# Gate columns moved into the value projection of a RetNet/HGRN2 layer, with the head norm along the free axis and a transpose at the end

## The chip, the cores and the metric

The kernel runs on one core of one Trainium2 chip. The metric is the device time in microseconds (us) of one execution. A NeuronCore has several engines that run side by side: PE (TensorE, the matrix products; PEld is the same engine loading the weights that stay put while the other operand moves), ACT (ScalarE), DVE (VectorE), POOL (GpSimd) and SP (SyncE, which here issues the DMAs). Products accumulate in PSUM banks; ACT and DVE read them from there ("evacuate" them) into SBUF.

## The reference

One layer of a hybrid decoder over 2048 prompt tokens and 64 sample tokens (8 sequences of 8 tokens, with a carried state), width 1024:

```python
proj = h @ w_in                       # h = rmsnorm(x); 8 parts of 512 columns
rq, rk, rv, rg, hq, hf, hi, hg = split(proj)
# four retention heads: rotary on rq, rk; chunked recurrence with a fixed decay
o_r, s_ret_new = chunk_gla(rq, rk, rv, log_gamma, s_ret)
o_r = head_rmsnorm(o_r, ret_norm_w) * silu(rg)
# four HGRN2 heads: f = lb + (1-lb) sigmoid(hf), k = 1-f, q = silu(hq)/sqrt(dk)
o_h, s_hg_new = chunk_gla(hq, 1 - f, hi, log(f), s_hg)
o_h = head_rmsnorm(o_h, hgrn_norm_w) * silu(hg)
x = x + concat([o_r, o_h]) @ w_out
x = x + square(relu(rmsnorm(x) @ w_up)) @ w_down        # d_ff = 4096
y = rmsnorm(x)
```

`head_rmsnorm(o, w)` is `o * rsqrt(mean(o*o over the head's 128 values) + 1e-6) * w`. The outputs are y and the new states of all heads, for the prompt and for each sample sequence.

## The kernel before, in words

**Precision.** Every float32 product is made of three products of a faster format: each operand is split into a high and a low part, and high x high, high x low and low x high are accumulated. A weight block is 128 x 1024 values (1024 = 8 blocks of 128 columns). `weight` (L244) loads a raw block from DRAM, ACT copies the high part (L270) and DVE subtracts for the low part (L284). The input and output projections' blocks from the fifth on are stored in DRAM as parts by the first group (`next_weight`, stores at L318) and loaded as parts by the other two (L253). Raw blocks have 3 buffers, blocks used by the Strassen sums 4 of their own tag, parts 3 pairs. `self.ahead` is 2: at a block's use the next two are begun.

**Stages.** The 2112 tokens are cut into three groups (L41) of 640, 768 and 704 tokens (64 of samples and 640 of the prompt). Each group is mixed in turn: 0 to 350 us, 350 to 760 and 760 to 1188 us. The feed-forward part of all three follows, to the end, with Strassen-Winograd products (L1211) whose weight sums are made during the mixing of groups 1 and 2 (`plan_sums`, L1232; loads L1240, stores L1248).

**Mixing.** `mix` (L623) runs over four pairs p, each of one retention and one HGRN2 head. For each it emits: the gates of the pair before (`gates`, L664); the projections f, q, rq, rk (`project`, L674); the recurrence (`mixer`, L860, by an agenda); and the values (`values`, L717). Gates and projections keep the weights still and move the tokens: a block gives a tile [128 columns of w_in x T tokens], in two halves of T/2 tokens (L341). A gate is evacuated by DVE with the row norm, sigmoided by ACT (with loads of an activation table before and after) and multiplied. The values keep a 128-token chunk still and move the weights: 8 x 3 matmuls of 256 columns (both heads' 128, L748) per chunk. For the 64 sample tokens the two high products share one stationary tile, whose lower half holds the low part of the tokens; the lower rows are then moved by a DMA and added (16 matmuls, L742, L744). Up to three chunks share a PSUM tile; ACT evacuates a chunk with the token's norm factor as the scale (L758).

**Order.** Engine orders come from the emission order and a tile scheduler. `at`, `later` and `tick` (L206 to L222) form an agenda: `tick` is called once per few matmuls of projections and values, and what is due is emitted between them. `mixer` puts its steps at written offsets: scores by levels of blocks, then per chunk `outputs` (L1100, L1102) and `states` (L1108, L1115) 7 ticks apart. In the last group the sample sequences come ahead of the chunks: `sample_states` (L769) loads 4 states per buffer and two buffers per head, `sample_out` (L781, L784) multiplies, `sample_update` (L835, L839, L842, L843) makes the new states and stores them from the same buffers. The load buffers (`ld`, 6) also hold cos and sin for a whole group and the low copies.

**Head norm and output.** Outputs lie as [128 values x tokens], in one PSUM bank per segment and head. `gate_norm` (L1183) squares on ACT (L1188), splits the squares, multiplies output by gate (L1190), sums over the 128 partitions by two matmuls with a tile of ones (L511, L512), takes rsqrt on ACT (L357, L358) and multiplies (L1196). `cut_heads` (L1199) splits the gated heads in two parts, which `residual` (L1216) and `out_proj` (L1262) use as the moving operand of the output projection. PSUM: two double banks `pj` for projections and values, four banks `mm` for all small products.

Of the kernel before, what the change touches and what calls it, by code (L numbers as in the profile page):

```python
# [9 lines left out]
F32 = mybir.dt.float32  # L10
F32R = mybir.dt.float32r
# [18 lines left out]
NSLAB = 44  # L30
NLD = 6
# [19 lines left out]

N_MADE = 4
# [94 lines left out]
def in_blocks():  # L147
    for p in range(H):
        if p:
            yield from ((7, p - 1), (3, p - 1))  # L150
        yield from ((5, p), (4, p), (0, p), (1, p), ("v", p))
    yield from ((7, H - 1), (3, H - 1))


def lay_out_weights(w_in, w_out, w_up, w_down):
# [3 lines left out]
    for part, p in in_blocks():  # L159
# [4 lines left out]
        for half in range(2):  # L164
            b = wi[half * 4:half * 4 + 4][:, :, (2, 6), p]
            w[i] = b.transpose(1, 0, 2, 3).reshape(P, WT)
            i += 1
# [32 lines left out]
class Kernel:  # L200
# [43 lines left out]
    def weight(self, i):  # L244
        n = len(self.stream)
        while self.w_next < min(i + 1 + self.ahead, n):
            j = self.w_next
            e = self.stream[j]
            if e[0] == "p":

                self.wts[j] = tuple(self.wp.tile([P, WT], F32R, tag=tag, name=tag) for tag in ("hi", "lo"))
# [16 lines left out]
            hi = self.wp.tile([P, WT], F32R, tag="hi", name="hi")  # L268
            lo = self.wp.tile([P, WT], F32R, tag="lo", name="lo")
# [353 lines left out]
    def mix(self, g):  # L623
# [6 lines left out]
        prev = None  # L630
        end = 0
        for p in range(H):
            b = {}
            if prev is not None:
                self.gates(g, prev)
            self.project(g, p, b)
            end = self.mixer(g, p, b, max(self.now, end))
            self.values(g, p, b)
            prev = b
        for p in range(H - 1):  # L640
            self.later(2 + 18 * p, self.cut_heads, g, p)
        self.gates(g, prev)
# [21 lines left out]
    def gates(self, g, b):  # L664

        for key, col in (("gh", V_HN), ("gr", V_RN)):
            z = self.normed(g, self.block(g))
            sg, q = self.get(), self.get()
            self.sigmoid(sg[:, :g.T], z)
            b[key] = q  # L670
            self.later(5, lambda q=q, z=z, sg=sg, col=col: self.nc.vector.scalar_tensor_tensor(
                out=q[:, :g.T], in0=z, scalar=self.vec[:, col:col + 1], in1=sg[:, :g.T], op0=ALU.mult, op1=ALU.mult))
# [44 lines left out]
    def values(self, g, p, b):  # L717

        nc = self.nc
        w = [self.next_weight(), self.next_weight()]  # L720
        b["vs"], b["vc"] = None, []

        left = -(-len(g.starts) // 3)
        i1 = 0
        while left:
            i0, i1 = i1, i1 - (i1 - len(g.starts)) // left
            left -= 1
            part = g.starts[i0:i1]
            pj = self.pj.tile([P, 2, 512], F32, tag="pj", name="pjv").rearrange("p a b -> p (a b)")
            v = self.get()  # L730
            for i, s in enumerate(part):
                for kb in range(KB):
                    hh, hl = g.h[kb]
                    cols = slice((kb % 4) * 256, (kb % 4 + 1) * 256)
                    wh, wl = w[kb // 4][0][:, cols], w[kb // 4][1][:, cols]
                    if g.ns and s == 0:

                        dst = pj[:, i * 256:(i + 1) * 256]
# [8 lines left out]
                    for q, (a, ww) in enumerate(((hh, wh), (hh, wl), (hl, wh))):  # L747
                        nc.tensor.matmul(pj[:, i * 256:(i + 1) * 256], a[:, s:s + C], ww,  # L748
                                         start=kb == 0 and q == 0, stop=kb == KB - 1 and q == 2)
                    self.tick()  # L750
                pair = (v[:, i * 256:i * 256 + P], v[:, i * 256 + P:(i + 1) * 256])
# [1076 lines left out]
```

## Time and profile before

| | us |
|---|---|
| median of 3 runs | 2494.79 (2494.51 to 2495.32) |
| span of the profiled execution | 2490.7 |
| what lies around the span, by the median | 4.1 |
| mixing of group 0, 1, 2 | 350, 410, 428 |
| feed-forward part | 1302 |

In the profile a row of a view that groups instructions reads: line, engine, operation, output<-input by the program's names, partitions x elements, count, then busy time and the mean or the min/median/max in ns of one. In the chain of work that ended last, a row is start, length, engine, tile and line, with the count of instructions in that piece. A row of DMA issues ends with the median time from issue to landing in us. In the timeline, "x2" means that two instructions of the kind follow each other in that row. Matmuls overlap on PE, so that their durations add up to more than the time that they take.

### The profile page before, as it was taken

What the parts mean: (1) busy time and instruction counts of PE and PEld (TensorE: products, weight loads), DVE (VectorE), ACT (ScalarE), POOL (GpSimd) and SP (SyncE); (2) the same over time, 40 slices, a digit from 0 to 9 for tenths busy, and PEclk for the clock granted to TensorE, in tenths of its full rate; (3) what the DMA queues carried; (4) which work ended last, traced back from release to release, by engine and by line L of the source; (5) the groups of instructions that cost most, each with busy time, mean ns of one, the idle gap of its engine ahead of it and who ended that gap; (6) DMA issues with size and microseconds to landing.
All of it is one profiled execution on the core that took longest, in us unless ns stands there. A gap on an engine that the chain in (4) does not pass through costs nothing.

```text
span 2490.7 us, 41430 instructions
## 1 busy us (share of the span) xinstructions
PE 2478.4 (100%) x16520; PEld 2461.9 (99%) x16520; DVE 1868.8 (75%) x2453; ACT 1246.4 (50%) x1674; POOL 377.3 (15%) x320
## 2 busy tenths in 40 slices
PE   9999999999999999999999999999999999999998
PEld 9999999999999999999999999999999999999998
DVE  7666766667685666686775899776699878778987
ACT  6665663444464444453644545444454436445544
POOL 5223304324421442340000000000000000000000
PEclk9999999999999999999999999999999999999999
DMA  7454575465566665768876866576675545867552
GB/s 265 166 185 170 203 259 178 161 229 186 184 210 236 220 219 200 266 211 270 283 213 221 280 198 213 174 239 222 203 262 177 188 151 190 288 196 247 194 189 89
DMA packets 191655, 525.44 MB, mean 211 GB/s; under 512 B 20963, under 2 KB 62563, under 8 KB 191462
## 3 DMA queue, kind: packets, MB, share of 16 engines
q1 hardware_dynamic: 191318, 522.77, 62.3%
q8 instruction: 130, 2.13, 0.4%
q14 instruction: 63, 0.52, 0.1%
q10 hardware_dynamic: 144, 0.02, 0.0%
HBM read 389.28 MB, written 132.39 MB: 209 GB/s over the span
## 4 chain that ended last, share of the span: by engine, by line
PE 98%; DVE 1%; DMA 0%; ACT 0%; issue 0%; SPq 0%; DVEq 0%
PE pj L341 29%; PE pf L1211 26%; PE pj L1211 25%; PE pjv L748 8%; PE mm L920 2%; PE mm L1108 1%; PE po L1100 1%; PE po L1102 1%; PE mm L977 1%; PE mm L512 1%; PE mm L511 1%; PE po L784 1%; PE mm L1034 1%; PE mm L850 1%; DMA lo<-w33lo 0%; DMA slab<-x 0%
## 5 line engine op out<-in xcount | busy, mean ns | idle before, releaser
L270 ACT CAST hi<-raw 128x1024 fp32r<-128x1024 f32 x392 | 411.8, 1050 | 616.6 <-PE pf L1211 258.4
L341 PE MATMUL pj<-slab,hi 128*128 128x320 f32 (+2 forms) x3072 | 661.4, 328 | 1.8 <-DVE slab L649 1.0
L1211 PE MATMUL pf<-slab,hi 128*128 128x320 f32 (+2 forms) x2768 | 657.6, 321 | 0.0
L1211 PE MATMUL pj<-slab,hi 128*128 128x352 f32 (+2 forms) x2608 | 620.6, 322 | 0.0
L284 DVE TENSOR_TENSOR lo<-raw,hi 128x1024 fp32r<-128x1024 f32 x392 | 485.6, 1239 | 113.6 <-ACT hi L270 108.1
L341 PEld LDWEIGHTS pj<-slab,hi 128*128 128x128 f32 x3072 | 508.3, 188 | 3.9 <-DVE slab L649 1.2
L1211 PEld LDWEIGHTS pf<-slab,hi 128*128 128x128 f32 x2768 | 480.1, 188 | 0.0
L1211 PEld LDWEIGHTS pj<-slab,hi 128*128 128x128 f32 x2608 | 452.9, 188 | 0.1
L1211 PE MATMUL pf<-slab,lo 128*128 128x320 f32 (+2 forms) x1384 | 444.1, 321 | 0.0
L1211 PE MATMUL pj<-slab,lo 128*128 128x352 f32 (+2 forms) x1304 | 419.1, 321 | 0.0
L341 PE MATMUL pj<-slab,lo 128*128 128x320 f32 (+2 forms) x1536 | 379.5, 327 | 0.5 <-DVE lo L284 0.4
L341 PEld LDWEIGHTS pj<-slab,lo 128*128 128x128 f32 x1536 | 263.6, 188 | 1.6 <-DVE lo L284 1.0
L1211 PEld LDWEIGHTS pf<-slab,lo 128*128 128x128 f32 x1384 | 259.6, 188 | 0.0
L1211 PEld LDWEIGHTS pj<-slab,lo 128*128 128x128 f32 x1304 | 244.6, 188 | 0.0
L748 PE MATMUL pjv<-hi,slab 128*128 128x256 f32 x1024 | 193.3, 285 | 0.0
L1302 ACT CAST slab<-slab 128x640 fp32r<-128x640 f32 (+2 forms) x192 | 145.2, 778 | 64.0 <-DVE slab L1313 51.7
L1306 DVE TENSOR_TENSOR slab<-slab 128x640 fp32r<-128x640 f32 (+2 forms) x192 | 167.0, 884 | 8.5 <-PE pj L1211 2.8
L748 PEld LDWEIGHTS pjv<-hi,slab 128*128 128x128 f32 x1024 | 162.2, 192 | 1.4
L748 PE MATMUL pjv<-lo,slab 128*128 128x256 f32 x512 | 144.8, 283 | 0.0
L899 ACT ACTIVATE slab<-slab 128x640 f32<-128x640 f32 (+2 forms) x72 | 56.3, 782 | 147.7 <-POOL slab L895 147.4
L1556 DVE TENSOR_TENSOR slab<-pf,slab 128x640 f32<-128x640 f32 (+2 forms) x88 | 77.5, 886 | 29.4 <-PE pf L1211 28.9
L748 PEld LDWEIGHTS pjv<-lo,slab 128*128 128x128 f32 x512 | 98.1, 192 | 0.0
(222 smaller groups left out, 3009.0 us busy)
## 6 DMA issues: line engine op xcount, KB each, us to landing
raw<-w SPq DMA_DIRECT2D x264, 512.0 KB, 4.3
slab<-u SPq DMA_DIRECT2D x32, 384.0 KB, 4.8
u<-ld SPq DMA_DIRECT2D x30, 384.0 KB, 4.0
slab<-u SPq DMA_DIRECT2D x32, 352.0 KB, 5.0
u<-ld SPq DMA_DIRECT2D x30, 352.0 KB, 3.9
slab<-u SPq DMA_DIRECT2D x32, 320.0 KB, 4.6
u<-ld SPq DMA_DIRECT2D x30, 320.0 KB, 4.3
ld<-x SPq DMA_DIRECT2D x16, 384.0 KB, 3.8
```

The source lines that it names most:

```text
L270: self.nc.scalar.copy(hi, raw)
L284: self.nc.vector.tensor_tensor(out=lo, in0=self.second.pop(j), in1=hi.bitcast(F32), op=ALU.subtract)
L341: self.nc.tensor.matmul(pj[:, i, :T2], w, a[:, c0:c1], start=j == 0 and q == 0, stop=j == n - 1 and q == 2)
L511: self.nc.tensor.matmul(ps, self.ones_r, hi, start=True, stop=False)
L512: self.nc.tensor.matmul(ps, self.ones_r, lo, start=False, stop=True)
L748: nc.tensor.matmul(pj[:, i * 256:(i + 1) * 256], a[:, s:s + C], ww, start=kb == 0 and q == 0, stop=kb == KB - 1 and q == 2)
L899: nc.scalar.activation(x["dd", w][:, a:T], x["dd", w][:, a:T], AF.Exp)
L920: nc.tensor.matmul(ps[:, j], qk[:, cols[c]], second(qk[:, cols[c]]), start=True, stop=True)
L1211: self.nc.tensor.matmul(*a, **k)
L1302: self.nc.scalar.copy(hi[:, :g.T], B[name][:, :g.T])
L1306: self.nc.vector.tensor_tensor(out=lo[:, :g.T], in0=B[name][:, :g.T], in1=hi.bitcast(F32)[:, :g.T], op=ALU.subtract)
L1556: nc.vector.tensor_tensor(out=r, in0=ps, in1=r, op=ALU.add)
```

## The change

- The weights are laid out anew: a pair's value blocks hold 512 columns per 128 rows (value and gate of both heads), four blocks per pair instead of two (`N_VAL`), and the two gate blocks are gone. The count of blocks stays.
- `values` moves 512 columns in place of 256. Two chunks share a `pj` tile. ACT evacuates values and gates with two copies per chunk. The sample chunk's lower rows are moved and added for values and gates.
- `gates` works on [tokens x gate columns] slabs: sigmoid as Exp, Ln, Exp on ACT (no table load), then a product on DVE.
- `outputs` and `sample_out` swap their operands, so that outputs lie as [tokens x 256 (both heads)]; two chunks share a bank of `mm`.
- The head norm sums squares along the free axis: ACT Square with an accumulated sum per token (`squares`), Ln and Exp on a [128, 2, 2] tile (`factors`), one DVE operation per chunk and head that multiplies output, factor and gate (`gated`).
- `cut_heads` transposes the gated heads back by PE, 128 x 128 at a time; ACT and DVE make the parts from PSUM with the norm's weight as the scale. Heads 0 to 2 are cut 50, 65 and 80 ticks after the last `mixer` is begun.
- Buffers: slabs 44 to 43, load buffers 6 to 5, raw weight blocks 3 + 4 to 4 of one tag, part pairs 3 to 5.

The diff, cut:

```diff
-NSLAB = 44
-NLD = 6
+NSLAB = 43
+NLD = 5
+NRAW = 4
+NPART = 5
+N_VAL = 4
 def in_blocks():
     for p in range(H):
-        if p:
-            yield from ((7, p - 1), (3, p - 1))
         yield from ((5, p), (4, p), (0, p), (1, p), ("v", p))
-    yield from ((7, H - 1), (3, H - 1))
...
-                k, later = self.w_load, self.w_load >= self.n_sums
-                other = later and k % 7 % 2
-                raw = self.raws[k] = self.wp.tile([P, WT], F32, tag="sum" if other else "raw", name="raw",
-                                                  bufs=4 if other else 3)
+                raw = self.raws[k] = self.wp.tile([P, WT], F32, tag="raw", name="raw", bufs=NRAW)
...
-            if prev is not None:
-                self.gates(g, prev)
             self.project(g, p, b)
             end = self.mixer(g, p, b, max(self.now, end))
+            if p == H - 1:
+                for q in range(H - 1):
+                    self.later(50 + 15 * q, self.cut_heads, g, q)
             self.values(g, p, b)
...
+    def gates(self, slab, n, first):
+        nc, sg = self.nc, self.get()
+        z, e = slab[:, :n], sg[:, :n]
+        self.later(first, lambda: nc.scalar.activation(e, z, AF.Exp, scale=-1.0))
+        self.later(first + 3, lambda: nc.scalar.activation(e, e, AF.Ln, bias=1.0))
+        self.later(first + 6, lambda: nc.scalar.activation(e, e, AF.Exp, scale=-1.0))
+        self.later(first + 11, lambda: nc.vector.tensor_tensor(out=z, in0=z, in1=e, op=ALU.mult))
...
+        ahead, self.ahead = self.ahead, NPART - N_VAL
+        w = [self.next_weight() for _ in range(N_VAL)]
+        self.ahead = ahead
...
+        for j0 in range(0, n, 2):
+            pj = self.pj.tile([P, 2, 512], F32, tag="pj", name="pjv")
...
+                    cols = slice((kb % 2) * 512, (kb % 2 + 1) * 512)
...
+                        nc.tensor.matmul(dst, a[:, s:s + C], ww, start=kb == 0 and q == 0, stop=kb == KB - 1 and q == 2)
+                        if q != 1:
+                            self.tick()
...
-        nc.tensor.matmul(po[:, :NS], v, AT, start=True, stop=False)
+        nc.tensor.matmul(po, AT, v, start=True, stop=False)
...
-                nc.tensor.matmul(dst, b["vc"][c][hd], am(i, c), start=True, stop=first)
+                nc.tensor.matmul(dst, am(c), b["vc"][c][hd], start=True, stop=first)
                 if not first:
-                    nc.tensor.matmul(dst, S, qd[:, cols[c]], start=False, stop=True)
+                    nc.tensor.matmul(dst, qd[:, cols[c]], S, start=False, stop=True)
...
+        def squares(k, i, c, r=slice(0, P)):
+            o, _ = place(c)
+            for hd in range(2):
+                a = hd * P
+                nc.scalar.activation(o[r, a:a + P], x["po", k][r, i * 256 + a:i * 256 + a + P], AF.Square,
+                                     accum_out=x["ss", k][r, hd, i:i + 1])
...
+        for c in range(n):
+            two, i = divmod(c, 2)
+            at(t + 6, outputs, c)
+            at(t + chunk, states, c)
+            at(t + 9, squares, two, i, c)
+            if i or c == n - 1:
+                at(t + 9, factors, two, i + 1)
+                for d in range(i + 1):
+                    at(t + 13 + d, gated, two, d, c - i + d)
+            t += chunk
...
     def cut_heads(self, g, p):
...
+                    nc.tensor.transpose(ps[:, s:s + n], o[:n, c:c + P], self.ident[:n, :n])
+                self.tc.keep_in_program_order(nc.scalar.activation(hi[:, a:e], ps, AF.Copy, scale=w))
+                nc.vector.scalar_tensor_tensor(out=lo[:, a:e], in0=ps, scalar=w, in1=hi.bitcast(F32)[:, a:e],
+                                               op0=ALU.mult, op1=ALU.subtract)
```

More of the change, by code (lines that the diff above doesn't have):

```diff
@@ L163, in lay_out_weights @@
             continue
-        for half in range(2):
-            b = wi[half * 4:half * 4 + 4][:, :, (2, 6), p]
+        for two in range(N_VAL):
+            b = wi[two * 2:two * 2 + 2][:, :, (2, 6, 3, 7), p]
             w[i] = b.transpose(1, 0, 2, 3).reshape(P, WT)
@@ L747, in values @@
                     for q, (a, ww) in enumerate(((hh, wh), (hh, wl), (hl, wh))):
[L748 to L751, printed above, removed]
-                if g.ns and s == 0:
-                    b["vs"], b["vrows"] = pair, v[:NS, :2 * P]
-                else:
-                    b["vc"].append(pair)
@@ L756, in values @@
-            for i in range(len(part)):
-                cc = slice(i * 256, (i + 1) * 256)
-                nc.scalar.activation(v[:, cc], pj[:, cc], AF.Copy, scale=g.rt[:, i0 + i:i0 + i + 1])
-                if g.ns and part[i] == 0:
-                    rows, low = v[:NS, cc], self.load()[:NS, :2 * P]
-                    nc.sync.dma_start(low, v[NS:, cc])
-                    self.later(16, lambda rows=rows, low=low: nc.vector.tensor_tensor(out=rows, in0=rows, in1=low, op=ALU.add))
+                        nc.tensor.matmul(dst, a[:, s:s + C], ww, start=kb == 0 and q == 0, stop=kb == KB - 1 and q == 2)
```

152 lines of the change are left out of this document (79 added, 73 removed).

## The prediction

> **What bounds the kernel now.** I read the head of the page first (span, busy time per engine), then its chain of work that ended last, then the busy time per engine in four windows: one for the mixing of each token group and one for the feed-forward part.
>
> ```profile
> span 2490.7 us, 41430 instructions
> PE 2478.4 (100%) x16520; PEld 2461.9 (99%) x16520; DVE 1868.8 (75%) x2453; ACT 1246.4 (50%) x1674; POOL 377.3 (15%) x320
> PE 98%; DVE 1%; DMA 0%; ACT 0%; issue 0%; SPq 0%; DVEq 0%
> ```
> ```profile
> 0.00:350.20 350.20, 347.90 (x2593) 342.63 (x2593) 252.83 (x412) 222.38 (x332) 113.71 (x100) 1.00 0.56 197
> 350.20:760.00 409.80, 409.80 (x2814) 405.24 (x2815) 281.88 (x410) 191.90 (x281) 133.14 (x100) 1.00 0.57 201
> 760.00:1188.00 428.00, 427.01 (x3025) 421.76 (x3024) 284.37 (x472) 193.85 (x308) 130.42 (x120) 1.00 0.69 237
> 1188.00:2490.00 1302.00, 1293.68 (x8093) 1292.24 (x8091) 1049.70 (x1160) 638.30 (x756) 0.00 (x0) 1.00 0.64 210
> ```
> In the windows the columns are window, length, then busy time of PE, PEld, DVE, ACT, POOL, the granted clock and the DMA share. PE is busy for 347.9 of 350.2, 409.8 of 409.8 and 427.0 of 428.0 us in the three mixing stages, always at clock 1.00, and 98% of the chain is PE. No other engine (PEld is PE's own weight load) is over 73% busy in a mixing stage. So the end is set by the sum of PE's own work, and the change is worth what it takes from that sum, less every new moment in which PE stands. The change touches the first three windows; the fourth is touched only through its weight buffers.
>
> Matmuls overlap, so a duration is no price; the price is the distance from one start to the next. The chain gives it: a piece with its length and its count of matmuls.
>
> ```profile
> 36.95 14.03 PE pjv L748 x117
> 811.75 0.12 PE pjv L744
> 813.58 11.15 PE pjv L748 x93
> 1392.87 7.04 PE pj L1211 x48
> 1607.94 8.32 PE pj L1211 x48
> 2273.40 7.63 PE pj L1211 x48
> ```
> L748 has 256 columns: 14.03/117 = 119.9 ns. The pieces of L1211 have 320, 384 and 352: 146.7, 173.3 and 159.0 ns. All are columns/2.4 plus 12.4 to 13.3 ns. The same products at L341 have the same widths.
>
> **The change part by part.**
>
> *Gates into the values' products.* Before, a head's gates are two blocks of 8 x 3 x 2 pieces = 96 matmuls with half a group's tokens moving (320, 384, 352), and its values 24 matmuls of 256 columns per 128-token chunk (5, 6 and 5 chunks; in the last group also 16 for the 64 sample tokens, 0.12 each by L744). After, the same number of values' matmuls carry 512 columns. The nearest rows for 512 are two matmuls of 512 columns in the sample states:
>
> ```profile
> 866.32 0.46 PE mm L835 x2
> 869.87 0.52 PE mm L835 x2
> ```
> that is 230 to 260 ns, over 96 rows and in pairs whose last one borders on other work; the line through 256 to 384 gives 512/2.4 + 13.3 = 226.7. I take 226.7 and keep 239.8 (two of 256: nothing saved by widening) as the upper end, 224 as the lower.
> Group 0: 96 x 146.7 + 120 x 119.9 = 28.47 us becomes 120 x 226.7 = 27.20: -1.27 per head. Group 1: 96 x 173.3 + 144 x 119.9 = 33.90 becomes 32.64: -1.26. Group 2: 96 x 159.0 + 136 x 119.9 = 31.57 becomes 136 x 226.7 = 30.83: -0.74. Four heads of each: **-13.1 us**.
>
> A rule of the Trainium skill speaks against this term: its page "TensorE: Matmul & The Clock Gate", section "Back-to-back issue gap", puts the isolated gap at full clock at N/2.4 + 2.5 ns. By it each of the 1152 matmuls that go would save 2.5 ns and not 13.3, 2.9 us in all. The pieces above, 13.3 ns at 320 and 384 columns, disagree with it; what it would do here as a mechanism is the third rival.
>
> *Head norm's column sums.* They go. The norms are counted by their squares, one per segment and head:
>
> ```profile
> L1188 ACT ACTIVATE slab<-po x48: 377/487/496, 87.9 to 1149.3; 128x384 f32<-128x384 f32 x32, 128x256 f32<-128x256 f32 x8, 128x320 f32<-128x320 f32 x8
> 211.93 0.12 PE mm L511
> 213.04 0.17 PE mm L511
> 839.87 0.15 PE mm L511
> ```
> Each has two such matmuls (L511, L512), at 0.17 us for 384, 0.12 for 256, 0.15 for 320: 2 x (32 x 0.1733 + 8 x 0.12 + 8 x 0.1467) = **-15.4 us**.
>
> *Transposes at the end.* 128 x 128 each, one per chunk and head: (10 + 12 + 12) x 4 = 136. The kernel has such transposes already (keys, L850), and the sample outputs' matmuls stand beside them:
>
> ```profile
> 859.24 0.33 PE mm L850 x3
> 859.89 0.17 PE po L781 x2
> 860.06 1.79 PE po L784 x16
> ```
> 0.11 us each: **+15.0 us**. The sample outputs swap roles: their 16 matmuls moved 64 columns over 128 rows and paid 112 ns each, as much as 128 columns do, so they stay; the two of L781 (0.17) become as long as a 128-column pair (0.22): **+0.4** over 8 calls. Outputs of prompt chunks stay at 128 moving columns: 0.
>
> PE's work alone: -13.1 - 15.4 + 15.0 + 0.4 = **-13.1 us**. Now the waits, counted in the built program's order of instructions per engine, which holds no times.
>
> *First head's weights.* Values now need four weight blocks where two stood, all within the first chunk: blocks w6 and w7 after 12 and 18 matmuls (2.7 and 4.1 us) from 36.95.
>
> ```profile
> 27.99 0.42 SPq L233 DMA_DIRECT2D raw<-w  x1
> 28.59 0.51 ACT L357 ACTIVATE slab<-mm,eps 128x320 f32<-128x320 f32 x1
> 40.23 1.05 ACT L270 CAST hi<-raw 128x1024 fp32r<-128x1024 f32 x1
> 44.24 1.20 DVE L284 TENSOR_TENSOR lo<-raw,hi 128x1024 fp32r<-128x1024 f32 x1
> raw<-w SPq DMA_DIRECT2D x264, 512.0 KB, 4.3
> ```
> In the built order the cast of w6 stands on ACT between the two halves of the first norm factor (28.59), and its raw load is the one issued at 27.99, behind the store of w4's low part. With a landing of 3 to 4.3 us it comes at 31 to 32.3, so ACT, and behind it all that leads to the first head's sigmoids and copies, slips by about 2.9 us. The cast of w7 stands behind those copies, where 40.23 is now: without the slip it ends at 41.3 and DVE's low part at 42.5, with it at 44.2 and 45.4. Needed at 41.0 to 41.2: late by 1.3 to 4.2. I take **+3.0**, near the end that the order shows.
>
> *Sample states of group 2.* Five load buffers in place of six. In the built order the second half of the HGRN2 state of heads 0 to 2 takes the buffer of the first retention half, whose store must have landed:
>
> ```profile
> 867.21 1.28 DVE L839 SCALAR_TENSOR_TENSOR ld<-ld,mm 128x512 f32<-128x512 f32 x2
> L843 SPq DMA_DIRECT2D ret_so<-ld x8: 388/388/389, 867.9 to 1130.6; - x8
> DMA to landing us min/median/max: 2.6/3.3/4.8
> L769 SPq DMA_DIRECT2D ld<-hg_s x8: 384/424/943, 856.0 to 1116.6; - x8
> DMA to landing us min/median/max: 3.1/4.5/6.5
> ```
> (The second and third row of the fence are the store's, the last two the load's.) DVE 0.64, store issue and landing 0.4 + 3.3, load 4.5: 8.8, with semaphores some 8.9 us, against 8.2, 7.5 and 7.5 us of PE work that stand between the update's matmul and the first product that reads the state. PE waits 0.7 + 1.4 + 1.4: **+3.5** (0 with the shortest landings, 14 with the longest). SP's queue stands behind that load; what is queued there, the next weight blocks, is needed later than the state.
>
> *What I cost at nothing, and its cover.* (a) Low copies, sample rows: read 14 ticks later. (b) ACT gets the evacuation by halves, three passes over a gate's slab and two squares per chunk, but loses half its table loads and the gates' sigmoids; DVE loses the norm's splits and gets the gated products. By the windows DVE has 97 us or more and ACT 127 us or more free in each of these stages; without that cover nothing hides them. (c) Weight loads of groups 1 and 2 for the third and fourth value block stand when the preceding block's buffer is free, 7.3 to 12.6 us of PE work ahead of use in the built order. The landings of such loads in the trace go from
>
> ```profile
> hi<-w28hi SPq DMA_DIRECT2D x2, 512.0 KB, 3.2
> hi<-w24hi SPq DMA_DIRECT2D x2, 512.0 KB, 9.8
> ```
> (60 groups have a time; the long ones are w8, w16, w24, w32, the first projection of a head, issued beside other traffic). The third and fourth value block are late only if they land like those: this is the second rival. (d) In the feed-forward part a raw weight is loaded 12.3 us ahead of its cast where 20.2 stood, but cast 15.4 us ahead of its product where 7.7 stood; 27.7 in all for 27.9, against 4.3 for a landing: no change.
>
> Sum: -13.1 + 3.0 + 3.5 = **-6.6**, a span of 2484.1. The median of the runs shown, 2494.8, is 4.1 over the profiled span of 2490.7, so about **2488 us**.
>
> **The rivals.**
>
> *One: small waits in each output pair.* Two chunks' outputs now share one accumulator tile, and PE's matmuls for the second chunk write beside what ACT is still to square from the first. There are 7 pairs per head and four heads, 28, with 2.7 to 3.6 us of PE work between the two chunks; in 16 of them the squares stand in ACT's order only 0.3 to 0.5 us of PE work ahead. The squares of L1188 take 0.49 us for 384 columns; what stands ahead of them on ACT can be a cast of 1.05 (row above). Also the tiles stay held until DVE's gated products have read them, and four serve all small products. For it: the order. Against it: ACT is only half busy. At 0.25 us a pair it costs 7.0 us: 2495. From 0.18 a pair on the gain is below 0.2%.
>
> *Two (slower): the value weights come late in every head.* Four blocks instead of two must be there within 4.1 us of the values' start, in all 12 heads, and the buffers that receive the last two come free only as the blocks ahead end. If the fourth lands like w24 (9.8) where its lead is 7.3, PE waits 2.5 us, in the worst case twice. Against: before's shortest leads are as short, and PE shows no stall there. After the two waits that I count, 6.6 us of gain are left, so it turns the sign from 0.55 us per head and is slower by over 0.2% from 0.97; at 3 us per head it gives 2488 + 36 = 2524, at 1.5 it gives 2506.
>
> *Three: the wide matmul is no cheaper per column.* If the 13.3 ns are no constant per instruction, and 512 columns cost between 230 (L835) and 239.8 ns, the 1600 wide matmuls cost 5 to 21 us more: 2493 to 2509. For it: L835's 0.23 to 0.26. Against: three widths on one line.
>
> *Four: the sample states at the upper end of their landings.* 4.8 and 6.5 us in three heads make 14 where I take 3.5: 2499; and the second retention half, whose load stands only 4.8 us of PE work ahead of its use in the built order, would then be 1.7 us late in four heads: 2505. Against it: the medians, 3.3 and 4.5.
>
> That the change does not do what it says I leave out: the built program holds 14488 matmul instructions where 15600 stood.
>
> **How the numbers follow.** A measurement of this kernel tells about 0.2%, 5 us, from no change: faster is below 2489.8, slower above 2499.8. The forecast (2480 to 2490, by the ends of its two waits) gets 0.43, and an undisturbed sum without any wait (2481 and below) 0.02 more. Rival one gets 0.25, two 0.16, three 0.07 and four 0.07. Rival one, and the lower ends of three and four (0.05 together) fall within 0.2%: same 0.30. Two and the rest make slower 0.25, faster 0.45. The range goes from 2479 (no wait at all, and 224 ns for 512 columns) to 2506 (value weights 1.5 us late in each head; rival three's middle); what is above it, most of rival two, is about 0.14.
>
> **What would show it.** The values' piece of the chain that begins near 37 us should hold matmuls 227 ns apart; 240 would make rival three right. A transpose in the last stage of each group should cost 0.11. PE should stand about 3 us near 41 us, and 1 to 2 us ahead of the second half of the HGRN2 state's products in three heads of group 2, with a DMA into a load tile as releaser. If instead the idle time ahead of L1108's successor (the outputs, released by ACT's squares) adds up to over 5 us, rival one is right; if it stands ahead of the values' matmuls in groups 1 and 2 with a weight DMA as releaser, rival two. The fourth window's length should stay at 1302 within 2 us; if it grows, the claim on the shared weight buffers is wrong. The largest single risk is the count of small waits, since PE has none of them before.

## The result, and the profile after

The changed kernel takes **2503.9 us** (2501.8 to 2504.4 in 6 runs) where the kernel before takes 2494.6 on the same chip: a ratio of 1.0037 (95% interval 1.0025 to 1.0048), 9.3 us slower. The forecast was 2488 and faster; the time lies inside the range given, on the other side of no change. The two profiled executions lie further apart, 11.2 us (spans 2501.9 and 2490.7): the one of the kernel before took some 2 us less than its median, since in nearly every run that has both on record the time is 1.7 to 1.9 us over the span.

The head of the page of the changed kernel, then its busy time in windows cut at its own stages (columns as before; the second number of a row is the stage's length):

```profile
span 2501.9 us, 39554 instructions
PE 2481.5 (99%) x15408; PEld 2379.1 (95%) x15408; DVE 1814.2 (73%) x2449; ACT 1221.5 (49%) x1966; POOL 380.1 (15%) x320
...
PE 92%; DVE 2%; POOL 2%; DMA 1%; ACT 1%; issue 1%; SPq 0%; DVEq 0%; POOLq 0%; ACTq 0%
```
```profile
0.00:352.20 352.20, 346.61 (x2216) 318.13 (x2216) 243.36 (x406) 211.73 (x414) 115.29 (x100) 1.00 0.54 196
352.20:762.60 410.40, 408.76 (x2457) 376.55 (x2458) 257.74 (x410) 185.85 (x385) 130.19 (x100) 1.00 0.56 201
762.60:1199.10 436.50, 431.92 (x2646) 391.98 (x2645) 267.03 (x476) 187.68 (x417) 134.61 (x120) 1.00 0.66 229
1199.10:2501.00 1301.90, 1294.23 (x8093) 1292.41 (x8091) 1046.04 (x1158) 636.25 (x754) 0.00 (x0) 1.00 0.63 210
```

The feed-forward part is 1301.9 long where it was 1302.0: untouched. The mixing stages are 2.0, 0.6 and 8.5 us longer. The chain still is mostly PE, but DVE, POOL, DMA and ACT now hold 6% of it where they held 1%: others set the pace in places. (That share is no price: 6% of the span is 150 us, and far less was lost.) Note that "PE busy" hides most of this. A matmul that starts late under the tail of the one ahead leaves no idle time in the row, so it is the distance from start to start that tells.

So I summed, for both traces, the distances from start to start of all matmuls ahead of the feed-forward part, and took off a clean pitch for each: columns/2.4 + 13.3 ns for projections, values and column sums, the middle pitch within a row of its own kind for the small products.

| mixing, us | before | after | difference |
|---|---|---|---|
| clean work on PE | 1163.7 | 1151.2 | -12.5 |
| everything over it | 23.2 | 46.8 | +23.6 |
| sum | 1186.9 | 1198.0 | +11.1 |

The saving that was forecast for PE (-13.1) is there. It is more than paid back by time over the clean work. Split by the place where it shows, that +23.6 is: head 0's start 5.1; sample-state products 4.2; transposes of the gated heads 6.5; diffuse pitch of the 512-column matmuls 3.3; outputs and states 2.3; score products that break into the values 2.1; retention scores behind ACT's copies 1.5; the rest, of both signs, -1.4. The split is of one execution each, and neighbours run into each other in it by some tenths of a us.

The larger of them stand in the list of PE's waits (engine, tile and line, releaser, us in total, times, longest):

```profile
PE pjv L745 <- DVE slab L705: 3.4, 1, 3.4
PE mm L1229 <- DVE slab L1041: 1.8, 1, 1.8
PE mm L790 <- DMA ld<-hg_s: 1.6, 2, 1.4
PE mm L1040 <- ACT AT L986: 1.3, 3, 0.6
PE mm L406 <- DVE eps L410: 1.1, 1, 1.1
PE pj L339 <- DVE slab L1300: 0.8, 1, 0.8
PE mm L1110 <- DVE S L1123: 0.6, 1, 0.6
```

L745 is the values, L1229 the transposes, L790 the sample products, L1040 the retention scores. The two rows of L406 and L339 have their like in the kernel before, whose longest wait in this list is the first of them:

```profile
PE mm L408 <- DVE eps L412: 1.1, 1, 1.1
```
The waits of L1040 stand in group 1. Near 502 us ACT is idle for POOL, in its order ahead of the copy (L986) that PE needs:

```profile
501.09 0.85 ACT L905 ACTIVATE slab<-slab 128x768 f32<-128x768 f32 x1 [2.09 <-POOL slab L901]
501.84 0.51 ACT L986 COPY AT<-mm 64x192 f32<-64x192 f32 x2
```

**Head 0 of group 0.** PE, ACT, POOL and DVE of the changed kernel around 40 us, in four timelines (start, length, instruction, count, idle time before it and its releaser), then two rows of the kernel before:

```profile
36.57 0.46 PE L339 MATMUL pj<-slab,lo 128*128 128x320 f32 x2
40.37 0.50 PE L745 MATMUL pjv<-hi,slab 128*128 128x512 f32 x1 [3.35 <-DVE slab L705]
...
41.88 1.05 PE L745 MATMUL pjv<-hi,slab 128*128 128x512 f32 x2
```
```profile
28.67 0.51 ACT L355 ACTIVATE slab<-mm,eps 128x320 f32<-128x320 f32 x1
33.08 1.05 ACT L268 CAST hi<-raw 128x1024 fp32r<-128x1024 f32 x1 [3.91 <-DMA raw<-w]
34.03 0.47 ACT L356 ACTIVATE slab<-slab 128x320 f32<-128x320 f32 x1
```
```profile
34.58 4.32 POOL L592 TENSOR_TENSOR ld<-ld,slab 128x640 f32<-128x640 f32 x2 [10.62 <-ACT slab L356]
```
```profile
34.16 1.23 DVE L282 TENSOR_TENSOR lo<-raw,hi 128x1024 fp32r<-128x1024 f32 x1 [5.19 <-ACT hi L268]
35.30 4.28 DVE L643 TENSOR_TENSOR slab<-slab 128x640 f32<-128x640 f32 x2
39.51 0.81 DVE L705 TENSOR_TENSOR slab<-pj,ld 128x640 f32<-128x640 f32 x1
```
```profile
29.13 0.47 ACT L358 ACTIVATE slab<-slab 128x320 f32<-128x320 f32 x1
35.02 0.81 DVE L712 TENSOR_TENSOR slab<-pj,ld 128x640 f32<-128x640 f32 x1
```
The cast of w6 stands between the two halves of the norm factor, as the built order showed, and waits for its load until 33.08. ACT slips by 4.9 us (L356 at 34.03; its counterpart L358 stood at 29.13). What PE then waits for is not a weight but DVE's L705, the query's rotary product, which frees the PSUM tile that the first values go to. It starts 4.5 us later than its counterpart L712 in the kernel before. What ended last ahead of it is DVE's own row of work, which follows the slip without a gap: the low part of w6 (L282), two products with the norm factor (L643, until 39.58), then L705. POOL multiplies the rotary tables by the factor too (L592, two products), and L705 reads the first of them; but that one was done by 36.8, and both by 38.9. After the stall most matmuls of 512 columns start 427 ns apart from 41.45 to 44.4, against 227 later; the granted clock in that stretch:

```profile
41.40:44.80 3.40, 3.40 (x9) 2.65 (x8) 1.12 (x2) 3.33 (x5) 3.26 (x3) 0.51 0.72 288
```
So after 3.66 us from the last start to the next come 3.4 us at half clock, 1.6 us more.

The changed kernel has a second such stretch, in group 2 at 1096 us, from the end of the burst of transposes (L1229) with the wait of 1.8 us:

```profile
1092.60:1096.05 3.45, 1.23 (x9) 0.76 (x8) 3.45 (x7) 1.11 (x2) 1.27 (x1) 1.00 1.02 321
1096.06:1099.46 3.40, 3.40 (x18) 2.49 (x16) 1.89 (x4) 1.51 (x4) 0.00 (x0) 0.50 1.00 366
```
It costs 1.8 us over the clean pitches, so that the half clock makes 3.3 us of the +23.6 in all. No single idle time of PE ahead of it was over 1.81 us, but PE was busy for only 1.23 of the 3.45 us. The Trainium skill, page "TensorE: Matmul & The Clock Gate", section "What's actually happening", says that PE falls back to 1.2 GHz after an idle window of about 3.4 us and needs one such window of work to recover. The time to recover agrees, 3.4 us both times; a window that is idle throughout was not needed here.

**Sample states.** SP and PE of the changed kernel in head 0 of group 2:

```profile
871.73 0.99 SPq L849 DMA_DIRECT2D ret_so<-ld  x2
...
874.54 0.39 SPq L775 DMA_DIRECT2D ld<-hg_s  x1
```
```profile
879.82 1.06 PE L790 MATMUL mm<-ld,slab 128*64 128x128 f32 x8 [1.38 <-DMA ld<-hg_s]
```
The load is issued 2.8 us behind the store and lands 5.1 later: the wait that the prediction counted. It stands in the list twice, 1.4 us in this head and 0.2 in the next. The rest of the 4.2 is mostly not a wait for a load: each of the eight bursts of sample products costs about 0.25 us over its own matmuls, where the kernel before has 0.11 in four and nothing in the others.

### The profile page after: what moved, and what is told of

Same layout as the page of the kernel before. It is cut to its first block, busy times and chain, and to the rows that moved or that the text cites. A ratio compares the mean times of both kernels' runs of the same rounds, so it can differ in the third digit from the quotient of the medians.

```text
span 2501.9 us, 39554 instructions
## 1 busy us (share of the span) xinstructions
PE 2481.5 (99%) x15408; PEld 2379.1 (95%) x15408; DVE 1814.2 (73%) x2449; ACT 1221.5 (49%) x1966; POOL 380.1 (15%) x320
## 4 chain that ended last, share of the span: by engine, by line
PE 92%; DVE 2%; POOL 2%; DMA 1%; ACT 1%; issue 1%; SPq 0%; DVEq 0%; POOLq 0%; ACTq 0%
PE pf L1240 26%; PE pj L1240 25%; PE pj L339 20%; PE pjv L745 12%; PE mm L926 2%; PE mm L1108 1%; PE mm L1110 1%; PE mm L1116 1%; DMA raw<-w 1%; PE mm L983 1%; PE mm L1229 1%; PE mm L856 1%; PE mm L790 1%; PE mm L1040 1%; POOL slab L901 0%
## 5 line engine op out<-in xcount | busy, mean ns | idle before, releaser
L282 DVE TENSOR_TENSOR lo<-raw,hi 128x1024 fp32r<-128x1024 f32 x392 | 482.9, 1233 | 120.8 <-ACT hi L268 116.0
L339 PE MATMUL pj<-slab,hi 128*128 128x320 f32 (+2 forms) x2304 | 486.6, 327 | 0.8 <-DVE slab L1300 0.8
L1240 PEld LDWEIGHTS pj<-slab,hi 128*128 128x128 f32 x2608 | 452.9, 188 | 0.1
L339 PEld LDWEIGHTS pj<-slab,hi 128*128 128x128 f32 x2304 | 382.0, 188 | 5.0 <-issue 1.9
L745 PE MATMUL pjv<-hi,slab 128*128 128x512 f32 x1024 | 349.1, 403 | 3.4 <-DVE slab L705 3.4
L339 PE MATMUL pj<-slab,lo 128*128 128x320 f32 (+2 forms) x1152 | 282.3, 326 | 0.1
L1240 PEld LDWEIGHTS pj<-slab,lo 128*128 128x128 f32 x1304 | 244.7, 188 | 0.0
L745 PEld LDWEIGHTS pjv<-hi,slab 128*128 128x128 f32 x1024 | 194.1, 190 | 40.3 <-DVE slab L705 3.6
L745 PE MATMUL pjv<-lo,slab 128*128 128x512 f32 x512 | 206.7, 404 | 0.0
L339 PEld LDWEIGHTS pj<-slab,lo 128*128 128x128 f32 x1152 | 198.3, 188 | 0.5 <-DVE lo L282 0.4
L745 PEld LDWEIGHTS pjv<-lo,slab 128*128 128x128 f32 x512 | 97.1, 190 | 15.3 <-DVE lo L282 0.3
```

What stands on the lines that cost most here:

```text
L282: self.nc.vector.tensor_tensor(out=lo, in0=self.second.pop(j), in1=hi.bitcast(F32), op=ALU.subtract)
L339: self.nc.tensor.matmul(pj[:, i, :T2], w, a[:, c0:c1], start=j == 0 and q == 0, stop=j == n - 1 and q == 2)
L745: nc.tensor.matmul(dst, a[:, s:s + C], ww, start=kb == 0 and q == 0, stop=kb == KB - 1 and q == 2)
L1240: self.nc.tensor.matmul(*a, **k)
```

## The experiments

Two theories stood against each other. **Waits**: the loss sits in named places and goes when each is mended. **Spread**: it is the cost of every break in the wide matmuls, and mending moves it elsewhere. Ratios are to the kernel before, on the same chip, with 95% intervals. The median of the kernel before lay between 2492.9 and 2494.6 on the chips used, so gains are taken from the ratios, not from the times. An interval reaches some 0.001 to each side, 2 to 3.5 us.

**cast.** The seventh block is begun one projection earlier in group 0:

```diff
         self.sigmoid(sg, sg)
+        if start:
+            self.ahead = 3
+            self.weight(3)
+            self.ahead = 2
```


> The changed kernel, with the high part of the seventh weight block (w6) made one projection earlier in group 0 only, so that ACT does it ahead of the first norm factor and its load stands ahead of the stores of w4. Theory (the loss sits in a few named waits): in the changed kernel ACT waited 4.4 us for w6 between the two halves of that factor, POOL's rotary tables slipped with it, the projection's PSUM tile came free late, and PE stood 3.5 us at 36.7 and then ran 3.4 us at half clock. With the cast moved the stall shrinks below 1 us and the slow stretch goes: 4 to 5 us off, about 2499 to 2500. Rival (the loss is spread over every interruption of the wide matmuls, the stalls only show it): under 1 us off, 2503 to 2504. Second rival (the prediction's own: PE waits for w7's low part near 41 us): w7's cast still stands behind the swapped copies, so 1.3 us or more of waiting stays near 41 us, 2500 to 2502.

Measured: 1.0020 (1.0012 to 1.0029), 2498.5 us; 0.0017 less than the changed kernel, 4.2 us; the two intervals just overlap. Of the 3.5 us stall at the values' start nothing is left, and the half clock behind it is gone. (The expectation puts the slip down to POOL's tables; by the rows above DVE's own work was later.) The second rival's wait shows as well, in the trace of cast:

```profile
43.73 0.50 PE L749 MATMUL pjv<-lo,slab 128*128 128x512 f32 x1 [0.95 <-DVE lo L282]
```
This is w7's low part, the wait that I had put in the prediction for this place; it is worth 1 us. Elsewhere cast has a stretch at half clock of its own, in group 2, behind two waits for DVE of 0.90 and 0.68 us in the output pairs:

```profile
1150.40:1153.70 3.30, 1.72 (x11) 1.34 (x10) 3.30 (x6) 0.81 (x2) 0.00 (x0) 1.00 0.48 166
1153.80:1157.10 3.30, 3.30 (x15) 3.30 (x14) 3.01 (x8) 1.98 (x8) 0.00 (x0) 0.50 0.96 315
```

**state.** A buffer of its own for the second half of each HGRN2 state:

```diff
+            self.st = ctx.enter_context(tc.tile_pool(name="st", bufs=1))
...
-            s = self.load()
+            s = self.st.tile([P, 512], F32, tag="st", name="st") if which and i else self.load()
```


> The changed kernel with a buffer of its own for the second half of each HGRN2 sample state (2 KB per partition), so that its load does not wait for a retention half's store. Theory: the 4.4 us of waits ahead of the second half of those products in group 2 (1.55 and 0.33 us the largest) go: 3 to 4.5 us off, 2499.5 to 2501. Rival (spread): PE waits as long elsewhere in group 2, since DVE and POOL are behind there: under 1 us off.

Measured: 1.0029 (1.0017 to 1.0040), 2500.3 us: about 2.0 us off by the ratios, under the 3 to 4.5 expected. The waits for the state's landing are gone from the list, so the place is right. One thing stood against the gain: the first of these loads, free to go at once, went third in SP's queue, ahead of seven of the eight loads of the first tokens. In the profiled execution of three PE then stands 1.5 us until 9.7 us, and 3.4 us at half clock begin there, 1.8 us more:

```profile
6.10:9.50 3.40, 1.64 (x9) 1.01 (x7) 1.39 (x2) 0.87 (x2) 0.00 (x0) 1.00 0.95 351
9.60:12.90 3.30, 3.19 (x10) 2.79 (x11) 3.23 (x5) 3.30 (x6) 0.00 (x0) 0.50 1.05 419
```

**cut.** The transposes of heads 0 to 2 in group 2 moved:

```diff
-                    self.later(50 + 15 * q, self.cut_heads, g, q)
+                    self.later(60 + 13 * q if g.ns else 50 + 15 * q, self.cut_heads, g, q)
```


> The changed kernel with the transposes of heads 0 to 2 in group 2 at 60, 73 and 86 ticks after the last mixer's start instead of 50, 65 and 80. Theory: their burst of four PSUM tiles at 1092 us met DVE 2 us behind (its work on the decays, with weight sums between), so PE stood 2.0, 0.6 and about 1 us more; 10 ticks later DVE has caught up: 2.5 to 4 us off, 2500 to 2501.4. Rival (spread, or the burst itself): four tiles that must all be free at once are late wherever the burst stands, under 1 us off or a like wait at the new place.

Measured: 1.0029 (1.0018 to 1.0039), 2500.2 us: about 2.0 us off. First the changed kernel, then cut, at the same place on PE:

```profile
1092.16 0.64 PE L1229 MATMUL mm<-con,slab 64*128 64x64 f32 x3
1094.61 0.55 PE L1229 MATMUL mm<-con,slab 128*128 128x128 f32 x3 [1.81 <-DVE slab L1041]
1095.57 1.25 PE L1229 MATMUL mm<-con,slab 64*128 64x64 f32 x6 [0.42 <-DVE AT L970]
```
```profile
1094.89 0.43 PE L1032 MATMUL mm<-slab 128*128 128x64 f32 x2 [0.43 <-DVE slab L1041]
...
1095.86 0.54 PE L983 MATMUL mm<-slab 128*32 128x32 f32 x12 [0.25 <-DVE AT L970]
...
1098.99 1.54 PE L1229 MATMUL mm<-con,slab 64*128 64x64 f32 x9
```
The stall in the burst goes, and the half clock behind it; the next products that need DVE's tiles wait 0.4 and 0.25 instead. DVE was late there, and the burst only met it first: part of the gain is given back, as the rival said. But the stall also shrinks where the transposes were not moved. In the trace of cast the same wait is this one (state has the same 0.29), with no half clock behind it:

```profile
1089.41 0.55 PE L1233 MATMUL mm<-con,slab 128*128 128x128 f32 x3 [0.29 <-DVE slab L1045]
```
So the 1.8 us is no fixed price of this place, and a gain of 2.0 that lies within the intervals doesn't show that the move brought it.

**three.** The three edits together.

> The three edits together. Theory: they are independent places, so 10 to 13 us off the changed kernel, 2491 to 2494, that is 0 to 4 us faster than the kernel before. Rival (spread): 0 to 3 us off, 2501 to 2504.

Measured: 1.0003 (0.9994 to 1.0012), 2494.3 us. That is 8.5 us under the changed kernel by the ratios, about the sum of the three (4.2 + 2.0 + 2.0) and under the 10 to 13 expected, and level with the kernel before. Taken alone, the 2.0 of state and of cut lie within the intervals; the gain of the three together does not. The theory of waits, with the half clock behind them, holds for a good third of the +23.6, at under its price. What remained over the clean work in this trace is 40.1 us, still 17 above the kernel before; the profiled execution is the slowest of the 11, by 2 us against the median, so some of the 17 is its own.

**late.** On top of the three edits, every score level 3 ticks later:

```diff
-        step, late, chunk, wait = 13, 24, 7, 14
+        step, late, chunk, wait = 13, 27, 7, 14
```


> The three edits, with every level of the scores 3 ticks later in each mixer (its offset 24 becomes 27). What is left over the kernel before's own waits is about 17 us in the three-edit kernel against 13 us saved on PE. Theory: several of these (scores under the values, 1.3 us; the waits for ACT's corner copies in group 1, 1.6 us; the later scores' tiles, 1.5 us) come from the chain of decays through POOL, ACT and DVE, which PE now reaches sooner since its own work is shorter; given 3 ticks, about 1 us, more, 2 to 3 us go: ratio to the three-edit kernel 0.9990, about 2490 where that has 2492.5 to 2494.3. Rival: the extra cost sits in PE itself (changes of the shape of the stationary tile next to 512 columns), and 3 ticks change less than 0.7 us.

Measured: 1.0001 (0.9992 to 1.0010): 0.5 us under three, within both intervals. The 2 to 3 us that the theory asked for do not show, though intervals of 2 us to each side can't exclude them. Against the theory speaks the trace: the three waits of the retention scores for ACT's copies stayed, at 1.6 us in the list.

**pad.** On top of the three edits, one shape of the stationary tile for the sample products:

```diff
-        nc.tensor.matmul(po, AT, v, start=True, stop=False)
...
-                nc.tensor.matmul(po, g.qm[i][:, s * NS:(s + 1) * NS], s0[i][:, s * P:(s + 1) * P],
-                                 start=False, stop=i == 1 and s == 3)
+                nc.tensor.matmul(po, g.qm[i][:, s * NS:s * NS + P], s0[i][:, s * P:(s + 1) * P],
+                                 start=i + s == 0, stop=i == 1 and s == 3)
+                if i + s == 0:
+                    nc.tensor.matmul(po[:NS], AT, v, start=False, stop=False, skip_group_check=True)
...
```


> The three edits, with the sample states' 16 products taking 128 columns of the masked queries as stationary instead of 64 (the upper rows of the result are not used), so that the stationary tile has the shape of the projections' tiles around it. Theory: each burst of these products costs 0.25 to 0.44 us over the sum of its matmuls in the three-edit kernel and 0.11 in the kernel before, because PE pays about 0.09 us for each change of the stationary tile's shape; with one shape 1 to 2 us go over the 8 bursts, and the burst's excess in the trace falls to 0.11 or less. The one matmul with the scores keeps 64 columns. Rival: the excess is a wait for the state's landing, and stays.

Measured: 1.0001 (0.9992 to 1.0010), no change that can be told. In the trace five of eight bursts cost 0.23 us over their matmuls where they cost 0.25: the one product that kept 64 columns, put second, is still in each. The other three, which run on into the update of the states, fell from 0.44 to between 0.09 and 0.15, some 1.0 us together, the lower end of the expectation. The times can't tell 1 us, and the price of 0.09 for each change of shape, on which the theory rests, is shown by no run: what causes the excess stays open.

**twice.** On top of the three edits, every transpose is done twice.

> The three edits, with every transpose of the gated heads done twice into the same place (result unchanged). It prices the 136 transposes: by 0.11 us each 15.0 us more than the three-edit kernel, 2507 to 2509.5. If part of them lay in time in which PE stood anyway, less: 8 to 12 us; if the burst of four tiles is what costs, the same 15, since the tiles are not held longer than by the work itself.

Measured: 1.0059 (1.0045 to 1.0073), 2508.1 us; 0.0056 over three, 14.0 us, for 15.0 by pitch. The term holds, within the 4 us to each side that the two intervals leave.

**sums2.** The kernel before with the head norm's column sums doubled.

> The kernel before, with the head norm's column sums done twice (added up, and the mean taken over twice the count: result unchanged). It prices what the change removed there: by the pitches 15.4 us more than the kernel before. Rival: PE had slack at these places, under 12 us more.

Measured: 1.0060 (1.0048 to 1.0073), 2508.7 against 2493.3 on that chip: 15.4 us. The pitch gave 15.4 too; the interval runs from 12 to 18 us. So these two terms cancel within what the runs can tell: doing the head norm along the free axis with a transpose is worth about nothing on PE.

**more.** The waits that were left in three, four edits in one run (on top of pad):

```diff
-            self.ahead = 3
+            self.ahead = 4
...
-                    self.later(60 + 13 * q if g.ns else 50 + 15 * q, self.cut_heads, g, q)
+                    self.later(60 + 13 * q if g.ns else 52 + 13 * q, self.cut_heads, g, q)
...
+            if which and i:
+                self.tc.keep_in_program_order(d)
...
-            at(46 + 4 * sg, ret_scores, sg)
+            at(48 + 4 * sg, ret_scores, sg)
```


> The padded three-edit kernel with the small waits that are left attacked one by one: w7's high part made early as well (a wait of 1.1 us at 42.7), the retention scores 2 ticks later (three waits of 0.5 to 0.7 us in group 1), the transposes of groups 0 and 1 at 52, 65 and 78 ticks instead of 50, 65 and 80, and the first sample state's load kept in its place in SP's order (in the three-edit kernels it went third in the queue, ahead of the first tokens, and the start waited 1 to 1.5 us). Theory (waits, each removable where it stands): 3 to 5 us off, a ratio to the kernel before of 0.998 to 0.9990, 2488.5 to 2490.5: the first version that is faster than the kernel before. Rival (what is left is spread and cannot be moved out): within 1 us of the three-edit kernel, 1.000.

Measured: 2488.7 us (2488.1 to 2490.4 in 11 runs), ratio **0.9980** (0.9971 to 0.9989): 5.6 us faster than the kernel before, and the fastest of all. Which of the four edits brought how much was not run apart. The granted clock is 1.00 through the whole mixing. In its list of waits none of the changed kernel's large ones is left:

```profile
PE mm L407 <- DVE eps L411: 1.0, 1, 1.0
PE pj L339 <- DVE slab L1308: 0.8, 1, 0.8
PE pj L339 <- ACT hi L268: 0.7, 1, 0.7
PE mm L1118 <- DVE S L1131: 0.7, 1, 0.7
PE pjv L750 <- DVE slab L710: 0.6, 1, 0.6
```
Its third mixing stage takes 426 us where the changed kernel's takes 436.5 and the kernel before's 428:

```profile
760.00:1186.00 426.00, 425.10 (x2632) 389.35 (x2631) 266.75 (x476) 187.34 (x415) 129.31 (x119) 1.00 0.67 236
```

**narrow.** Three, with each 512-column matmul of the values as two of 256:

```diff
-                        nc.tensor.matmul(dst, a[:, s:s + C], ww, start=kb == 0 and q == 0, stop=kb == KB - 1 and q == 2)
+                        for h in (0, 256):
+                            nc.tensor.matmul(dst[:, h:h + 256], a[:, s:s + C], ww[:, h:h + 256], start=kb == 0 and q == 0 and h == 0,
+                                             stop=kb == KB - 1 and q == 2 and h == 256, skip_group_check=True)
```


> The three edits, with each 512-column matmul of the values made as two of 256 with the same stationary tile. It prices the merging alone. By the clean pitches 2 x 119.9 against 226.7: 13.1 ns times 1536 = 20.1 us more than the three-edit kernel, 2513 to 2514. If the wide form costs more than its clean pitch where small products break in (229 to 231 ns between breaks), less: 16 to 18 us. If merging saves only 2.5 ns per matmul, as a constant part of that size would have it: 4 us.

Measured: 1.0045 (1.0031 to 1.0058), 0.0042 over three: 10.5 us, below the 16 to 20 that I expected by the clean pitch and above the 4. The chain shows that the pitches themselves are as forecast, here in the changed kernel (227.2 ns) and in narrow (119.9):

```profile
114.19 13.18 PE pjv L745 x58
```
```profile
111.89 13.91 PE pjv L751 x116
```
But over its clean work narrow has 27.6 us in the mixing, where three has 40.1.

**narrow2.** The same edit on the kernel of more.

> The kernel of the run more, with each 512-column matmul of the values made as two of 256, as in narrow. In narrow the merging proved to be worth 0.0042 of the time (10.5 us) where the clean pitches give 20.1. Theory A: the missing half is waits that come back as PE gets faster (in the trace the three-edit kernel has 12 us more of them than narrow); in more most of these waits are gone, so here the difference should be larger, 14 to 17 us, a ratio to the kernel before of 1.0036 to 1.0048. Theory B: the wide form itself costs that much where small products break in; then the difference stays at 10 to 11 us, a ratio of 1.0020 to 1.0026.

Measured: 1.0036 (1.0022 to 1.0050), 2502.9 us; 0.0056 over more, 14.0 us. That is the lower end of theory A: with the waits mended, merging would be worth 14 us instead of 10.5, of 20 by the pitches. But the intervals of the two differences overlap, and the traces do not bear out the ordering. The 40.1 of three are of its slowest execution; against the profiled execution of pad, which has no half clock, the mixing of narrow is 12.5 us longer, and that of narrow2 is 13.3 longer than that of more. So theory A is not shown against theory B. Of the 7 us still missing (over clean work, 33.2 us in more and 26.0 here), 4 lie in the values' stream itself: between two breaks the wide matmuls stand some 229 ns apart instead of 226.7 (in the timeline 228 to 236 for the first ones behind a break), and the narrow ones 119.9. That much is theory B.

## Why the prediction was wrong

- **What bounds the kernel, and PE's own work: right.** -13.1 forecast, -12.5 in the trace. The column sums (-15.4) and the transposes (+15.0) came out at 15.4 and 14.0 by doubling each; the clean pitch of 512 columns at 227.2 for 226.7. The last step, 4.1 us from the span to the time, was 1.7 to 1.9 in nearly every run: the other 2 us came from a profiled execution that was quicker than the median.
- **First head's weights: right place, half the mechanism.** +3.0 forecast, 5.1 measured (4.2 by taking it away). The slip of ACT behind w6's load was as read from the order, at 4.9 us for 2.9. What it held up was the PSUM tile, through DVE's work behind the norm factor, not w7's low part, which alone costs 1 us; that 3.0 stood near the 3.5 us of the stall is luck. The half clock behind the stall, 1.6 us, was not in the sum.
- **Sample states: right place, half the size.** +3.5 forecast for waits in three heads; the trace has 1.6 us of them in two, and taking them away gave 2.0. The 4.2 in the table's split comes near 3.5 only because it holds the bursts' own 0.25 us each, which the prediction put at no extra cost.
- **"What I cost at nothing, and its cover" is the step that failed**, and with it the forecast that only two waits are added. The cover was taken from each engine's share of busy time in a stage (97 us of DVE free, 127 of ACT). The transposes met DVE in the one place where it was 2 us behind (6.5 us over their clean work in the trace, with some of the 1.8 us of half clock); the retention scores met ACT, which stood idle itself, waiting for POOL with the copies behind it (1.5). That is 8 us of failed cover. The first term failed by less: it priced the wide matmuls at their clean pitch, without the breaks, and they lost 3.3 by their pitch, and by the scores breaking in 2.1. Together some 13 us that stood in no term, against the 6.6 that were to be gained. Mending waits brought the kernel from 1.0037 to 0.9980, 14 us, more than the 9.3 that were lost: that waits, with the half clock behind them, are the cause is shown. The size of each item is read from one trace.
- **Rival one** was the right family with the wrong member: small waits ate the gain. But the pairs of outputs that it named cost 2.3 us and not 7, and ACT's squares held up PE's weight loads (PEld) for only 1.8 us:

```profile
L1136 ACT ACTIVATE slab<-mm x136: 254/271/279, 92.0 to 1161.0; 128x128 f32<-128x128 f32 x128, 64x128 f32<-64x128 f32 x8
...
  PEld mm L1108: 1.8, 6
```
(The first row are the squares; the second is from the part of the same answer that tells who waited for them: 1.8 us in 6 of 28 pairs.)

- **Rival two (value weights late in every head): wrong.** The only wait of the values for a weight is one of 0.3 us, of a weight load in group 0.
- **Rival three (the wide matmul is no cheaper): part of the truth.** Its clean price is as extrapolated, yet merging saves 10.5 to 14 us of the 20 that this price gives.
- **Buffers of the feed-forward part: right**, 1301.9 for 1302.0.

What stays open: what makes the wide matmuls stand 2 to 3 ns further apart behind a break, how much of the transposes' 6.5 us is the shape of their tiles, and why the stall in their first burst of group 2 was 1.8 us in the changed kernel and 0.3 in cast and state. A separate output tile for each chunk wasn't tried.

## What to carry to other kernels

Where PE is full, saving 13 us of its work need not save 13 us: a chain through POOL, ACT and DVE that was just in time can now be late, so read for each moved product what its PSUM tile waits for, not how busy the engine is on average. The waits were single places that the built order showed (a cast that waits for a load in the middle of a norm, a load that waits for a store, a burst of four tiles), and mending them turned 0.4% slower into 0.2% faster. Waits that leave PE idle for half of some 3.4 us also put its clock at risk: four such places in these traces cost another 1.4 to 1.8 us at half clock. Price opposing terms by doubling each: two such runs showed that half of this change, the norm and its transposes, is worth about nothing.

## What the runs showed of the hardware that was not expected

- A stall of 3.66 us between two matmul starts brought 3.4 us at half clock (granted 0.51; 427 ns per 512 columns). So did shorter waits close together: in the 3.3 to 3.45 us ahead of the other stretches shown above PE was busy for 1.23 (the changed kernel at 1096 us), 1.72 (cast) and 1.64 us (three), with no idle time over 1.81, 0.90 and 1.54 us. Each stretch lasted 3.4 us and cost 1.4 to 1.8 us. At the place of the first stall cast has no wait over 0.95 us, and there the clock stayed at 1.00:

```profile
40.00:46.00 6.00, 5.05 (x23) 3.85 (x22) 5.11 (x9) 2.77 (x4) 2.23 (x2) 1.00 0.90 343
```
- The bursts of score products (L983), whose stationary tile has 32 or 64 columns, cost about 0.3 us each over their own matmuls, whatever stands around them: 15.4 us for 48 bursts before, 17.5 after, 15.3 in narrow. Most other breaks cost under 0.02 us each unless something is late; four each at L914 and L1026 of the kernel before cost 0.2. That the shape of the tile is the reason is not shown.
